# Attention's weights, copied bit for bit into rounded-kind tiles and transposed from there

## The chip, the cores and the metric

The kernel runs on one core of one Trainium2 chip. A core has TensorE (PE: matrix products and transposes, results into PSUM), VectorE (DVE), ScalarE (ACT) and GpSimd (POOL), each with its own queue of instructions, and SyncE (SP), whose queue here does nothing but issue transfers. The engines run in parallel and wait for each other by semaphores. Transfers are carried out by 16 DMA engines, whichever queue issues them. The metric is the device time of one execution in microseconds (us); lower is better.

## The reference, cut to what matters

One layer of a hybrid encoder on 1024 tokens of width 1024, all in float32. A normalised input feeds two branches, stick-breaking attention (8 heads of 64) and a gated linear recurrence (4 heads of 128); their gated sum goes through an output product, and then comes an MLP with a squared ReLU and a last normalisation. The change lies in the attention, of which the reference is:

```python
z = jnp.einsum('bhqd,bhkd->bhqk', qi, k) * scale
mask = kpos[None, :] < qpos[:, None]
log_beta = jax.nn.log_sigmoid(z)
log_rem = jnp.where(mask, log_beta - z, 0.0)
between = lax.cumsum(log_rem, axis=3, reverse=True) - log_rem
w = jnp.where(mask, jnp.exp(log_beta + between), 0.0)
return jnp.einsum('bhqk,bhkd->bhqd', w, v)
```

For a query t, the weight on key s is sigmoid(z_ts) times the product of (1 - sigmoid(z_tj)) over the keys j between s and t.

## The kernel before, in words

Everything is kept in float32, and most matrix products are built from a "rounded kind" of float32 (`F32R`): a number is split into a rounded high part and a low rest, and three products of the parts (`three`, L121 in the profile) stand for one full-precision product. A tile of the rounded kind has 4 bytes per element, like float32; an engine that writes such a tile rounds the values, and a transfer through a float32 view of it does not. In the profile's rows both kinds are often printed as f32.

The attention runs as 64 items, one for each of 8 heads (h) and 8 blocks of 128 queries (qb, in the order 7, 0, 6, 1, 5, 2, 4, 3). Item (h, qb) has nk = 128 (qb + 1) keys. It passes four steps, written two items apart from each other in the main loop:

1. `scores`: TensorE multiplies queries and keys into PSUM (`z`, 256 to 512 columns at a time, short ones padded to 256), and ScalarE takes two sigmoids of it, `rm` (L753) and `bt` (L756). GpSimd clears one column of `bt` (L757).
2. `weights`: VectorE scans `rm` backwards, which makes the running product (L775), and multiplies `bt` by it (L157). `bt` now holds the weights. For qb = 7 this is done in two parts, the upper 512 columns first (`cut`).
3. `turn`: TensorE transposes `bt` block by block, 128 x 128, against an identity matrix into PSUM banks `pw` (L124), up to four blocks a bank, 36 blocks a head, 288 in all. ScalarE copies each bank into `wT` (`hi_copy`, L144).
4. `values`: once a head's eight items are turned, TensorE multiplies `wT` with V into `po` (L121).

In iteration i of the main loop the program writes `weights` of item i + 1, `scores` of item i + 2, then some "fill" (the projections of later heads and of the recurrence: `pjqk`, `pjv`, `pji` and others, L121), then `turn` of item i. So a multiply of step 2 stands about one and a half items ahead of the transposes that need it. On TensorE the attention's blocks form one lane ("main") and the projections another ("fill"): within a lane the order is fixed, and a fill block may not run ahead of more than two main blocks. Beyond that a planner lays out each engine's order by the program's priorities and by when it reckons that an instruction is ready.

Weights for the projections come by `load` (L129) on SP's queue, in an order of their own; each waits for one of two buffers, which comes free when VectorE has split the weight before (L149). GpSimd's queue issues the small copies `QH<-QH` and `QL<-QL` (L661), which move 64 partitions of a tile to the other 64 inside the SBUF, and the transfers of the output weights (`tw`, L1195).

Tiles of up to 512 columns come from a pool of 10, wider ones from a pool of 40 slots of 4 KB per partition; a tile is given back after its last use, and a later one that finds no free slot waits.

Of the kernel before, what the change touches and what calls it, by code (L numbers as in the profile page):

```python
# [9 lines left out]
F32 = mybir.dt.float32  # L10
F32R = mybir.dt.float32r
# [8 lines left out]
P = 128  # L20
# [19 lines left out]
def kernel(  # L40
# [19 lines left out]
    nc = tc.nc  # L60
# [7 lines left out]
    cpool = ctx.enter_context(tc.tile_pool(name="consts", bufs=1))  # L68
# [6 lines left out]
    def slot(name, dt=F32):  # L75
        return spool.tile([P, 1024], dt, tag="s", name=name)

    def slot_n(name, n, dt=F32):

        if n <= 512:  # L80
            return hpool.tile([P, 512], dt, tag="h", name=name)
        return slot(name, dt)

    def bank(name):
        return psum.tile([P, 512], F32, tag="p", name=name)
# [12 lines left out]
    def after(ins, earlier):  # L98
        if earlier is not None and earlier.ins is not ins.ins:
            tc.add_manual_dep(ins.ins, earlier.ins.name, NOSYNC, reason="issue order")  # L100
        return ins

    def open_block(name):
        cur[0] = name
        lane = lanes[name]
        lane.gates = (lane.last,)
        if name == "main":
            lane.ends.append(lane.last)
        else:
            ends = lanes["main"].ends  # L110
            lane.gates += tuple(ends[-AHEAD : len(ends) - AHEAD + 1])

    def pe(ins):
        lane = lanes[cur[0]]
        for g in lane.gates:
            after(ins, g)
        lane.last = ins
        return ins
# [4 lines left out]
    def transpose(dst, src):  # L123
        return pe(nc.tensor.transpose(dst, src, ident))  # L124
# [18 lines left out]
    def hi_copy(dst, src):  # L143
        hi_last[0] = after(in_turn("act", nc.scalar.copy(dst, src)), hi_behind[0])  # L144
# [11 lines left out]
    def mul(out, a, b):  # L156
        return nc.vector.tensor_tensor(out=out, in0=a, in1=b, op=ALU.mult)  # L157
# [4 lines left out]
    ident = cpool.tile([P, P], F32, tag="ident", name="ident")  # L162
# [505 lines left out]
    def v_job(quad):  # L668
        unit = v_unit(quad)
        return st.add(  # L670
            [unit], lambda: token_steps(f"pjv{quad}", unit, xn, range(NT), v_epilogue(quad))
        )
# [51 lines left out]
    for h in range(1, NHS):  # L724
        j_qk[h] = proj_jobs([qk_item(h)], xn)
        if h == 4:
            v_job(1)

    QB_ORDER = (7, 0, 6, 1, 5, 2, 4, 3)
    items = [(h, qb) for h in range(NHS) for qb in QB_ORDER]  # L730
    zs, wTt, seen = {}, {}, {}
# [33 lines left out]
    def weights(h, qb):  # L765

        nk = (qb + 1) * P
        bt, rm = zs[h, qb]  # L770
        cut = qb == NT - 1
        parts = ((512, nk - 1), (0, 512)) if cut else ((0, nk - 1),)
        for i, (a, b) in enumerate(parts):
            rr = rm[:, a:b][:, ::-1]
            nc.vector.tensor_tensor_scan(  # L775
                out=rr,
                data0=rr,
                data1=bits[:, 1024 - nk + a : 1024 - nk + b][:, ::-1],
                initial=rm[:, b : b + 1] if i else 0.0,
                op0=ALU.mult,  # L780
                op1=ALU.max,
            )
            weighted[0] = mul(bt[:, a:b], bt[:, a:b], rm[:, a:b])

    def turn(h, qb, between):

        open_block("main")
        bt, rm = zs.pop((h, qb))
        qc, par = qb // 2, qb % 2
        nkb = 2 * qc + 2  # L790
        if (h, qc) not in wTt:
            wTt[h, qc] = [
                slot_n(f"wT{h}_{qc}_{k0}", 256 * min(nkb - k0, 4)).rearrange(
                    "p (k q) -> p k q", q=256
                )
                for k0 in range(0, nkb, 4)
            ]
        tiles = wTt[h, qc]
        qs = slice(par * P, (par + 1) * P)
        order = list(enumerate(tiles))  # L800
        for i, t in order[::-1] if qb == NT - 1 else order:
            n = min(qb + 1 - 4 * i, 4)
            if n <= 0:
                continue
            if qb == NT - 1 and i == 0:
                between()
                open_block("main")
            pw = bank(f"pw{h}_{qb}_{i}")
            for kb in range(n):
                s0 = (4 * i + kb) * P  # L810
                transpose(pw[:, kb * P : (kb + 1) * P], bt[:, s0 : s0 + P])
            hi_copy(t[:, 0:n, qs], pw[:, : n * P].rearrange("p (k q) -> p k q", q=P))
            turn_hi[0] = hi_last[0]
        seen[h] = seen.get(h, 0) + 1
        return (h,) if seen[h] == NT else None
# [1290 lines left out]
    st.advance(11, j_qk[0])  # L2106
    scores(*items[0])
    weights(*items[0])
    st.advance(1, j_qk[0])
    scores(*items[1])  # L2110
# [7 lines left out]
    for i, it in enumerate(items):  # L2118
        if i + 1 < len(items):
            weights(*items[i + 1])  # L2120
        if i + 2 < len(items):
            st.finish(j_qk[items[min(i + 4, len(items) - 1)][0]])
            scores(*items[i + 2])
        if i % 2 == 1:
            next(wsums, None)
        want = n_first + (i + 1) * (n_fill - n_first) // len(items)
        st.advance(want - done, j_hg[1])
        done = want
        before = ready.popleft() if ready else None

        def between():
            if before:
                values(*before)

        r = turn(*it, between)
        if i == len(items) - 2:
            attended[0] = weighted[0]
        if it[1] != NT - 1:
            between()
        if r:  # L2140
            ready.append(r)
# [127 lines left out]
```

## Time and profile before

| | us |
|---|---|
| median of 3 runs | 1431.91 (1429.53 to 1432.1) |
| the profiled execution | 1431.78 |
| its span, first to last instruction | 1430.0 |
| attention stage in it | 50 to 306 |

The profile's page gives the busy time of each engine, the span in 40 slices, the transfers by queue, the chain that ended last, and the costliest groups of instructions. A group's row names line, engine, operation, output tile and input tiles, shape and count, then total busy time, mean duration in ns, and how long the engine stood idle ahead of such an instruction. A matmul's duration holds the time that it takes to pass through the array, which overlaps the next one; how fast they follow each other is read from their starts.

### The profile page before, as it was taken

To read this page: it belongs to the slowest core of one execution; us is meant where nothing else is said; L and a number is where in the kernel's file an instruction comes from. 1 tells how busy PE (TensorE), PEld (TensorE's weight loads), DVE (VectorE), ACT (ScalarE), POOL (GpSimd) and SP (SyncE) were. 2 spreads that over 40 slices of the span, in tenths; PEclk is the share of its full clock that TensorE was granted. 3 is DMA by queue.
4 is the path that set the end of the run, shared out by engine and by line. 5 is a ranking of instruction groups with operands and counts; after the bars stand their busy time and mean duration, and the time that the engine had idled before them with its cause. 6 is when DMAs were issued, how large, how long until landed. Compare 5 with 4: busy or idle time off the path is not lost. (4 is left out here: it accounts for less than half of the span.)

```text
span 1430.0 us, 22381 instructions
## 1 busy us (share of the span) xinstructions
PE 1415.6 (99%) x8806; PEld 1189.1 (83%) x8806; DVE 1000.7 (70%) x1320; ACT 667.6 (47%) x1180; POOL 138.3 (10%) x283
## 2 busy tenths in 40 slices
PE   9999999999999999999989999999999999999998
PEld 8889888987888888888878888888888888888886
DVE  6577677655535677788758897766666758668765
ACT  7566676643322354432344764454444443524343
POOL 3121121110001022000010300000000000000042
PEclk9999999999999999999999999999999999999999
DMA  7235154312203458744487505444446974776725
GB/s 214 47 93 128 27 93 85 67 36 82 84 16 109 114 180 234 235 155 162 162 258 250 177 30 199 160 137 143 143 161 229 341 270 152 273 274 243 279 96 181
DMA packets 157920, 225.87 MB, mean 158 GB/s; under 512 B 25676, under 2 KB 93816, under 8 KB 157816
## 3 DMA queue, kind: packets, MB, share of 16 engines
q1 hardware_dynamic: 142552, 183.29, 38.1%
q0 software_dynamic: 11520, 34.61, 9.7%
q10 hardware_dynamic: 3744, 6.56, 1.2%
q8 instruction: 69, 1.13, 0.3%
q14 instruction: 35, 0.29, 0.1%
HBM read 162.55 MB, written 61.87 MB: 157 GB/s over the span
## 5 line engine op out<-in xcount | busy, mean ns | idle before, releaser
L775 DVE TENSOR_TENSOR_SCAN rm<-rm,bits 128x511 f32<-128x511 f32 (+7 forms) x72 | 87.9, 1225 | 47.7 <-ACT rm L753 47.6
L144 ACT CAST whid<-w 128x1024 fp32r<-128x1024 f32 x30 | 31.6, 1053 | 154.7 <-PE pm L121 86.8
L121 PE MATMUL pm<-wlod,sh 128*128 128x512 f32 x240 | 93.5, 390 | 0.0
L121 PE MATMUL pm<-whid,sh 128*128 128x512 f32 x240 | 93.4, 389 | 0.0
L121 PE MATMUL pm<-whid,sl 128*128 128x512 f32 x240 | 93.4, 389 | 0.0
L121 PE MATMUL pm<-tl,sh 128*128 128x512 f32 (+1 forms) x210 | 81.3, 387 | 0.0
L121 PE MATMUL pm<-th,sl 128*128 128x512 f32 (+1 forms) x210 | 81.3, 387 | 0.0
L121 PE MATMUL pm<-th,sh 128*128 128x512 f32 (+1 forms) x210 | 81.3, 387 | 0.0
L149 DVE TENSOR_TENSOR wlod<-w,whid 128x1024 fp32r<-128x1024 f32 x30 | 36.7, 1223 | 58.2 <-ACT whid L144 58.1
L149 DVE TENSOR_TENSOR sl<-sa,sh 128x1024 fp32r<-128x1024 f32 x56 | 68.2, 1218 | 0.5 <-ACT sh L144 0.5
L144 ACT COPY wT<-pw 128x512 f32<-128x512 f32 (+2 forms) x96 | 43.8, 484 | 45.5 <-PE pw L124 42.3
L144 ACT CAST sh<-sa 128x1024 fp32r<-128x1024 f32 x56 | 57.3, 1047 | 5.5 <-DMA sa<-ad 3.9
L1918 POOL TENSOR_SCALAR fss<-fss 128x1 f32<-128x1 f32 x8 | 4.5, 562 | 562.2 <-ACT fsc L1913 561.6
L157 DVE TENSOR_TENSOR bt<-bt,rm 128x511 f32<-128x511 f32 (+7 forms) x72 | 49.5, 690 | 9.1 <-ACT bt L756 3.0
L121 PEld LDWEIGHTS pm<-wlod,sh 128*128 128x128 f32 x240 | 45.0, 188 | 9.7 <-DVE wlod L149 0.4
L121 PEld LDWEIGHTS pm<-whid,sh 128*128 128x128 f32 x240 | 45.1, 188 | 9.4
L121 PEld LDWEIGHTS pm<-whid,sl 128*128 128x128 f32 x240 | 45.0, 188 | 9.4
L121 PE MATMUL pX<-sql,t1h 128*128 128x512 f32 x128 | 50.1, 391 | 0.1
L121 PE MATMUL pX<-sqh,t1l 128*128 128x512 f32 x128 | 49.9, 389 | 0.0
L121 PE MATMUL pX<-sqh,t1h 128*128 128x512 f32 x128 | 49.8, 389 | 0.0
L753 ACT ACTIVATE rm<-z 128x511 f32<-128x511 f32 (+4 forms) x96 | 48.3, 507 | 1.7 <-PE z L121 1.4
L756 ACT ACTIVATE bt<-z 128x512 f32<-128x512 f32 (+3 forms) x96 | 48.5, 507 | 1.2 <-PE po L121 0.9
(907 smaller groups left out, 4335.4 us busy)
## 6 DMA issues: line engine op xcount, KB each, us to landing
w<-in_w_ff_dram SPq DMA_DIRECT2D x72, 512.0 KB, 4.9
sa<-ad SPq DMA_DIRECT2D x56, 512.0 KB, 6.5
ad<-a SPq DMA_DIRECT2D x32, 256.0 KB, 4.2
ad<-s SPq DMA_DIRECT2D x16, 512.0 KB, 5.2
tw<-in_w_out_dram POOLq DMA_DIRECT2D x24, 256.0 KB, 4.3
x<-in_x_dram SPq DMA_DIRECT2D x8, 512.0 KB, 8.5
xnl<-xnh POOLq DMA_DIRECT2D x8, 512.0 KB, 9.4
pr<-pd SPq DMA_DIRECT2D x8, 512.0 KB, 6.2
```

The costliest lines, as they stand in the source:

```text
L121: return pe(nc.tensor.matmul(*a, **k))
L144: hi_last[0] = after(in_turn("act", nc.scalar.copy(dst, src)), hi_behind[0])
L149: nc.vector.tensor_tensor(out=dst, in0=src, in1=hi.bitcast(F32), op=ALU.subtract),
L157: return nc.vector.tensor_tensor(out=out, in0=a, in1=b, op=ALU.mult)
L753: nc.scalar.activation(rm[:, s0 + c0 - 1 : s0 + m - 1], z[:, c0:m], AF.Sigmoid, scale=-0.125)
L756: nc.scalar.activation(bt[:, s0 : s0 + e], z[:, :e], AF.Sigmoid, scale=0.125)
L775: nc.vector.tensor_tensor_scan(out=rr, data0=rr, data1=bits[:, 1024 - nk + a : 1024 - nk + b][:, ::-1], initial=rm[:, b : b + 1] if i else ...
L1918: nc.gpsimd.tensor_scalar(out=ssq, in0=ssq, scalar1=1.0 / D, scalar2=EPS, op0=ALU.mult, op1=ALU.add)
```

## The change

A second identity, `ident_r`, of the rounded kind is made once by ScalarE. At the end of `weights`, a tile `wr` of the rounded kind is taken, and one transfer on SP's queue (two for qb = 7, upper part first) copies `bt` into it, through a float32 view of `wr`. `turn` no longer reads `bt`: it transposes blocks of `wr` against `ident_r` into a rounded view of the same `pw` bank. The copies out of `pw` and all that follows are as before. `bt` and `rm` have their last use in `weights`.

```diff
+    ident_r = cpool.tile([P, P], F32R, tag="ident_r", name="ident_r")
+    nc.scalar.copy(ident_r, ident)
...
             weighted[0] = mul(bt[:, a:b], bt[:, a:b], rm[:, a:b])
+        wr = slot_n(f"wr{h}_{qb}", nk, F32R)
+        for a, b in ((512, nk), (0, 512)) if cut else ((0, nk),):
+            nc.sync.dma_start(wr[:, a:b].bitcast(F32), bt[:, a:b])
+        zs[h, qb] = wr
 
     def turn(h, qb, between):
 
         open_block("main")
-        bt, rm = zs.pop((h, qb))
+        wr = zs.pop((h, qb))
...
             for kb in range(n):
                 s0 = (4 * i + kb) * P
-                transpose(pw[:, kb * P : (kb + 1) * P], bt[:, s0 : s0 + P])
+                pe(
+                    nc.tensor.transpose(
+                        pw[:, kb * P : (kb + 1) * P].bitcast(F32R), wr[:, s0 : s0 + P], ident_r
+                    )
+                )
```

## The prediction

> **What bounds the kernel now.** I read the page first (busy shares, slices), then the busy times of the attention stage, then the groups of instructions in it, then single instructions in order of time.
>
> ```profile
> span 1430.0 us, 22381 instructions
> PE 1415.6 (99%) x8806; PEld 1189.1 (83%) x8806; DVE 1000.7 (70%) x1320; ACT 667.6 (47%) x1180; POOL 138.3 (10%) x283
> ...
> 50.00:306.00 256.00, 256.00 (x1682) 221.43 (x1682) 185.48 (x223) 168.88 (x399) 42.99 (x125) 1.00 0.36 75
> ...
> L124 PE MATMUL pw<-ident,bt 128*128 128x128 f32 x288 | 43.3, 273 | 0.0
> ```
>
> The third row is the stage from 50 to 306 us, in which all 64 attention items run; its columns are the length, then busy time and count of PE, PEld, DVE, ACT and POOL, the granted clock, the DMA share and GB/s. TensorE is busy for all 256.00 of 256 us at clock 1.00, VectorE for 185.48, ScalarE for 168.88. So TensorE bounds the stage, and time taken from it there should come off the end, as long as nothing else makes it wait. The last row is what the change touches: 288 transposes of `bt` (36 blocks for each of 8 heads), no idle time before them. Their 43.3 us of busy time is not their price, because matmuls overlap. The price is the step from one start to the next:
>
> ```profile
> 57.98 0.39 PE L121 MATMUL pjqk<-xnh,wqk1h 128*128 128x512 f32 x1
> 58.21 0.39 PE L121 MATMUL pjqk<-xnl,wqk1h 128*128 128x512 f32 x1
> ...
> 58.67 1.03 PE L124 MATMUL pw<-ident,bt 128*128 128x128 f32 x8
> ...
> 157.14 0.28 PE L121 MATMUL pjv<-wv1h,xnh 128*128 128x256 f32 x1
> 157.26 0.28 PE L121 MATMUL pjv<-wv1l,xnh 128*128 128x256 f32 x1
> ...
> 366.20 1.72 PE L121 MATMUL pkv<-v,pp 128*128 128x128 f32 x14
> ```
>
> Columns: start, duration, instruction. Eight transposes take 1.03 us, one alone 0.273: (1.03 - 0.273) / 7 = 0.108 us each (four in a row elsewhere, 0.60 us, give 0.109). 288 x 0.109 = 31.4 us of TensorE. The rounded-kind matmuls (`pjqk`, `pjv`; the trace prints them as f32) step 0.23 us at 512 columns and 0.12 at 256: 0.11 us for 256 columns, 0.43 ns a column, and about 0.01 us beside that. The transposes move 128 columns in 0.108, 0.84 ns a column: twice as long. That is what the change is after.
>
> **The change, part by part.**
>
> *The transposes.* Same count, same tile, but both operands of the rounded kind. No row shows such a transpose, so I bound it. Below: the columns at the rounded rate and nothing else, 128 x 0.43 = 0.055 us. Above, if the rounded kind brings that kind's slower weight load and this sets the step, the nearest row is `pkv`, full-precision 128-column matmuls with such loads: (1.72 - 0.275) / 13 = 0.111 us. The loads:
>
> ```profile
> L124 PEld LDWEIGHTS pw<-ident,bt 128*128 128x128 f32 x288 | 34.5, 140 | 6.7 <-issue 0.9 <-DVE QL L149 0.2 <-DVE osb L862 0.2
> L121 PEld LDWEIGHTS pji<-wi0h,xnl 128*128 128x128 f32 x64 | 12.2, 191 | 0.0
> L121 PEld LDWEIGHTS pkv<-v,pp x56: 187/192/192, 366.0 to 547.5; 128*128 128x128 f32 x56
> L121 PE MATMUL pkv<-v,pp x56: 270/275/275, 366.2 to 547.7; 128*128 128x128 f32 x56
> ```
>
> (Last two rows: durations as min/median/max.) A load of the same 128 columns takes 140 ns ahead of a transpose and 191 to 192 ahead of the others. The new instruction shares its operation with the 0.109 row and its kind with the 0.055 rate; being near to both, I take the middle, 0.083 us. It saves 288 x (0.109 - 0.083) = 7.5 us. Ends: 288 x 0.054 = 15.6 us saved, 288 x 0.002 = 0.6 us lost.
>
> *The copies.* 72 transfers on SP's queue, one for each multiply (two where `cut`): 288 x 64 KB = 18.9 MB, bit for bit from `bt` to `wr`. SP computes nothing, so issuing costs no engine. But each stands between the multiply (L157) that ends the weights and the transposes that need them, and its time to landing must fit into the slack there. I paired all 72 multiplies (first end at 54.1, last at 300.1 us) with the transposes of their item (58.7 to 305.3), in order: the slack runs from 2.37 to 11.88 us, median 6.0; 4 are under 3.3, 8 under 4.4, 23 under 5.4. The tightest two and a usual one:
>
> ```profile
> 106.69 0.81 DVE L157 TENSOR_TENSOR bt<-bt,rm 128x639 f32<-128x639 f32 x1
> ...
> 110.81 0.67 DVE L157 TENSOR_TENSOR bt<-bt,rm 128x511 f32<-128x511 f32 x1
> ...
> 168.03 0.83 DVE L157 TENSOR_TENSOR bt<-bt,rm 128x639 f32<-128x639 f32 x1
> ...
> 110.30 0.71 PE L124 MATMUL pw<-ident,bt 128*128 128x128 f32 x5
> ...
> 113.85 0.60 PE L124 MATMUL pw<-ident,bt 128*128 128x128 f32 x4
> ...
> 174.68 0.49 PE L124 MATMUL pw<-ident,bt 128*128 128x128 f32 x3
> ```
>
> 110.30 - 107.50 = 2.80; 113.85 - 111.48 = 2.37; 174.68 - 168.86 = 5.82 us. How long does a copy take?
>
> ```profile
> DMA packets 19854, 19.09 MB, mean 77 GB/s; under 512 B 7344, under 2 KB 15930, under 8 KB 19834
> ...
> QH<-QH POOLq DMA_DIRECT2D x14, 128.0 KB, 2.2
> ...
> wqk6r<-in_w_in_dram SPq DMA_DIRECT2D x2, 256.0 KB, 6.5
> ...
> wga0r<-in_w_in_dram SPq DMA_DIRECT2D x1, 512.0 KB, 3.8
> ...
> DMA to landing us min/median/max: 2.2/2.2/5.4
> ```
>
> The first four rows are of 58 to 306 us (the last column is us to landing), the fifth is of all transfers that touch `QH`. `QH<-QH` is the nearest: inside the SBUF, 128 KB, 2.2 us. The quietest load of 512 KB lands in 3.8. A line through both gives 2.7 us for 256 KB, 3.0 for 320, 3.3 for 384, 3.5 for 448. Against each item's own slack only the two tightest and one of 3.25 are late, by 0.3, 0.2 and 0.05 us: 0.6 us together. That is the low end. The stage's traffic doubles (19.09 MB before), and 110.9 us is just when `wqk6r` takes its 6.5 us, so the tightest item will land late by more; with 1.4 us for that I take 2.0 us of waiting. If every copy took 5.4 us, as the slowest `QH` did, the 23 items with less slack would lack 24.4 us in all (23 x 5.4 less their slacks, 99.8): the high end, since a TensorE that waits gives the next items time.
>
> *The queue it passes through.* Ahead of a copy on SP may stand a prefetched weight load that waits for its buffer:
>
> ```profile
> SPq L129 <- DVE wq1l L149: 30.5, 1, 30.5
> ...
> SPq L129 <- DVE wqk3l L149: 26.9, 1, 26.9
> ...
> 124.12 0.99 SPq L129 DMA_DIRECT2D wqk7r<-in_w_in_dram  x2
> 126.04 1.95 SPq L129 DMA_DIRECT2D wf0r<-in_w_in_dram  x1
> ...
> 181.18 0.37 SPq L129 DMA_DIRECT2D wq0r<-in_w_in_dram  x1
> ```
>
> These waits look dangerous, but SP stands there only because it ran ahead. In the program's order each such load comes after the instruction that it waits for, with two of the L157 multiplies between at the most; a copy behind it needs a multiply later on the same VectorE. I cost it at nothing; without that order a single such wait would be 20 us and more. The other way round, the loads now wait behind copies, so behind multiplies; they are issued a whole projection job ahead (the loads at 124.12 and 126.04 us are followed by the next at 181.18), and some us later do no harm. If the cover failed, ScalarE's split of that weight would be late next, then the fill matmuls.
>
> *Tiles.* `wr` takes one more tile per item, but `bt` now comes free when the copy lands and no longer when the transposes end. Both are held only while the copy flies, some 3 us. Late in the stage the 40 slots are full, and a new `bt` already waits for an older one's transposes:
>
> ```profile
> POOL bt L757 <- PE pw L124: 11.5, 1, 11.5
> ...
> L144 ACT COPY wT<-pw x96: 260/565/611, 59.4 to 305.6; 128x512 f32<-128x512 f32 x48, 128x128 f32<-128x128 f32 x16, 128x384 f32<-128x384 f32 x16, 128x256 f32<-128x256 f32 x16
> ```
>
> (First row: waits from 235 to 282 us, total, times, longest; second: all copies out of `pw`, min/median/max in ns.)
>
>
> TensorE is busy through that wait, so nothing now; what it costs if the cover goes is in the second rival. *The identity copy* is one ScalarE instruction of some 0.26 us (128 columns, as the smallest `wT` copies), once, on an engine idle for a third of the stage: nothing.
>
> **Sum.** The profiled execution took 1431.78 us (span 1430.0 and 1.8 around it), 0.13 under the median of 1431.91. 1431.8 - 7.5 + 2.0 = 1426.3 us. What cannot be told from no change is about 0.2%, 2.9 us: under 1429.0 is faster, over 1434.8 slower.
>
> **Rivals.** *One pass, fully.* The step is 0.055 to 0.06 us, and the wait stays: 1431.8 - 14.8 + 2.0 = 1419 us. For it: every rounded row in the trace goes at 0.43 ns a column. Against it: a bit-for-bit transpose must carry all 32 bits.
>
> *The transposes gain nothing.* Either all 32 bits need the two turns they take today, or the weight load sets the step at 0.111 us: 1431.8 + 0.6 + 2.0 = 1434.4 us, from 1432 to 1437, at the edge of slower. For it: the rounded kind's 191 ns loads. Against it: 140 ns for a load of the same bytes shows that a transpose's load differs. The Trainium skill, "TensorE: Matmul & The Clock Gate", section "LDWEIGHTS (loading the stationary operand)", has a load take its columns over 1.2 GHz, 107 ns here, and speaks for this rival; in its section "Terms" it calls transpose mode 4x faster for FP32 on weight loads, which speaks against it. The trace shows the short load of the f32 transpose, and cannot show that of the rounded one.
>
> *The copies come late (slower).* Place: the items that follow a big load or a projection's evacuation, as at 107 to 118 us. Price: at 4.4 us per copy the lacking slacks of the 8 tightest add up to 7.5 us, which eats the whole gain; from there on it loses, and at 5.4 us it is 1431.8 - 7.5 + 24.4 = 1449 at the most, some 1440 where half is won back by later slack. Held `bt` tiles in the full pool push the same way, since a late sigmoid makes a late multiply. For it: 6.5 us beside `wqk6r`, and 5.4 for one `QH`. Against it: 2.2 us is also the median. The Trainium skill, "DMA: Bandwidth & Descriptors", section "Issuing engines are not separate DMA queues", says that transfers issued from different engines share the same 16 DMA engines and interleave; by that rule SP's copies do meet POOL's transfers, and the 5.4 us row agrees.
>
> *A narrow rounded matmul is slow.* The kernel pads `z` to 256 columns (L121 `z` has no narrower row), as if less were no cheaper. If 128 columns fell to the full-precision rate, two records of 0.111 us: 288 x (0.222 - 0.109) = 32.5 us, 1466 us. Nothing in the trace shows a rounded matmul under 256 columns, so it can't be excluded.
>
> **How the numbers follow.** Forecast 42% (own range 1419 to 1430.5), full single pass 13%, no gain in the transposes 22%, late copies 14%, slow narrow kind 8%. Faster: 85% of the forecast and the single pass, 0.48. Same: the rest of the forecast and over half of the no-gain case, 0.20. Slower: the rest, 0.32. The range, 1417 to 1440, takes in the single pass, the no-gain case and the milder half of the late copies, and leaves out the slow narrow kind.
>
> **What would show it.** The step between `pw` starts: 0.083 right, 0.055, 0.11 or 0.22 a rival. The time to landing of `wr<-bt`: under 3.6 us right. TensorE's idle time before `pw`: 0 now, 2 us forecast; over 7 makes the third rival true. If the stage shrinks by the saving but the end does not move, I was wrong on TensorE as the bound; if weight splits wait for their loads, on SP's queue.

## The result: slower by 12.6 us

The changed kernel took 1443.33 us (median of 4 runs, 1442.83 to 1448.91); the kernel before, run beside it, took 1430.72 (4 runs, 1429.38 to 1432.1). The ratio is 1.0096, with a 95% interval of 1.0083 to 1.0109. That is 12.6 us slower, where 5.5 us faster was forecast, and outside the range of 1417 to 1440. Of the rivals, "the copies come late" (1440 to 1449) holds it.

### The profile after

First the page, then the busy times by stretch, with columns as in the prediction: length, PE, PEld, DVE, ACT and POOL, granted clock, DMA share, GB/s.

```profile
span 1441.4 us, 22689 instructions
...
PE 1413.5 (98%) x8806; PEld 1185.3 (82%) x8806; DVE 1000.3 (69%) x1320; ACT 668.0 (46%) x1181; POOL 132.3 (9%) x283
```

```profile
50.00:318.00 268.00, 254.72 (x1673) 217.71 (x1671) 185.00 (x223) 168.86 (x398) 42.95 (x125) 0.99 0.54 141
...
230.00:240.00 10.00, 10.00 (x49) 8.56 (x50) 4.49 (x6) 6.26 (x15) 0.86 (x3) 0.85 0.33 70
250.00:260.00 10.00, 7.61 (x66) 5.79 (x65) 3.50 (x3) 3.18 (x7) 1.09 (x5) 1.00 0.50 132
290.00:300.00 10.00, 9.81 (x80) 8.15 (x80) 5.56 (x8) 5.16 (x14) 1.88 (x6) 0.83 0.44 88
```

TensorE was busy for all 256 us of the stage before. Now the stage ends 13 us later and TensorE stands idle for 268.00 - 254.72 = 13.3 us of it. The granted clock, 1.00 throughout the stage before, falls to 0.85 and 0.83 in two of the slices. What the idle time waits for, and who else waits (the waits from 50 to 320 us: total, times, longest):

```profile
POOL bt L760 <- DMA wr<-bt: 34.0, 4, 10.9
...
PE pw L819 <- DMA wr<-bt: 11.6, 9, 3.2
...
ACT rm L756 <- DMA wr<-bt: 8.1, 2, 5.9
...
ACT bt L759 <- DMA wr<-bt: 5.6, 2, 5.4
...
PE pw L819 <- ACT bt L759: 1.7, 1, 1.7
...
SPq L129 <- DVE wq0l L149: 8.4, 1, 8.4
```

All ten waits of TensorE stand ahead of `pw`, nine of them for a copy by these rows (11.6 and 1.7 make up the 13.3 us). By the single records the tenth, 1.65 us at 103.68 us, is for one too: its copy landed at 103.54, and in each of the eight waits whose copy's landing the trace tells the transposes begin 0.14 us after it.

The transposes themselves, in groups and in order of time; the answering rows of before stand beside them, for the two `z` matmuls that follow each group:

```profile
L819 PEld LDWEIGHTS pw<-ident_r,wr x288: 137/140/183, 58.4 to 318.2; 128*128 128x128 f32 x144
L819 PE MATMUL pw<-ident_r,wr x288: 220/248/342, 58.7 to 318.2; 128*128 128x128 f32 x144
```

```profile
58.66 0.80 PE L819 MATMUL pw<-ident_r,wr 128*128 128x128 f32 x8
...
59.48 0.28 PE L121 MATMUL z<-KS,QL 128*128 128x256 f32 x1
...
62.35 0.22 PE L819 MATMUL pw<-ident_r,wr 128*128 128x128 f32 x1
...
62.70 0.39 PE L121 MATMUL z<-KS,QL 128*128 128x512 f32 x1
```

```profile
59.66 0.28 PE L121 MATMUL z<-KS,QL 128*128 128x256 f32 x1
...
62.53 0.27 PE L124 MATMUL pw<-ident,bt 128*128 128x128 f32 x1
...
62.87 0.39 PE L121 MATMUL z<-KS,QL 128*128 128x512 f32 x1
```

The step is (0.80 - 0.22) / 7 = 0.083 us, where it was 0.108. But from a group's start to the second `z` behind it, eight transposes take 59.48 - 58.66 = 0.82 us (0.99 before), and a single one 0.35 (0.34 before). So a group of one gains nothing: what is saved inside a group is in part lost on the way out of it, where the weight loads of the two `z` matmuls follow each other in 0.11 us in both kernels (59.37 after 59.26 here, 59.54 after 59.43 before). There are 71 groups in the order of TensorE, with 288 - 71 = 217 steps inside them. The group of eight gives 217 x 0.026 = 5.6 us as a first estimate.

The copies, in the transfers from 58 to 318 us (last column: us to landing), and over all of them:

```profile
DMA packets 29552, 37.27 MB, mean 143 GB/s; under 512 B 8474, under 2 KB 19733, under 8 KB 29529
...
tw<-in_w_out_dram POOLq DMA_DIRECT2D x23, 256.0 KB, 4.4
wr<-bt SPq DMA_DIRECT2D x22, 256.0 KB, 4.0
wr<-bt SPq DMA_DIRECT2D x8, 448.0 KB, 6.5
wr<-bt SPq DMA_DIRECT2D x8, 384.0 KB, 4.5
wr<-bt SPq DMA_DIRECT2D x8, 320.0 KB, 3.3
...
wr<-bt SPq DMA_DIRECT2D x7, 64.0 KB, 4.0
```

```profile
DMA to landing us min/median/max: 1.8/2.9/8.6
```

The stage's traffic has doubled. The copies take 4.0 us at 256 KB and 6.5 at 448, where 2.7 and 3.5 were reckoned; these are medians of the copies whose landing the trace tells, 40 of 72, and the slowest took 8.6 us. It is the slowest that cost most. Paired with their items, four waits (3.23, 2.40, 2.35 and 0.60 us, 8.6 of the 13.3) stand at items that had 6.35 to 8.5 us of slack in the kernel before, whose median was 6.2 (the prediction reads 6.0). The copies of three of them took 8.1 to 8.6 us, one of these a copy of only 64 KB; the fourth isn't told. The items with under 4.1 us of slack before have four of the waits, 3.8 us, and the tightest of all, with 2.37, has none. The longest wait shows how (in order of time):

```profile
217.10 1.09 DVE L157 TENSOR_TENSOR bt<-bt,rm 128x895 f32<-128x895 f32 x1
219.52 1.21 DVE L149 TENSOR_TENSOR wq0l<-wq0r,wq0h 128x1024 fp32r<-128x1024 f32 x1
...
220.43 0.91 POOL L1206 DMA_DIRECT2D tw<-in_w_out_dram  x1
220.79 0.37 SPq L129 DMA_DIRECT2D wi0r<-in_w_in_dram  x1
...
221.06 1.19 POOL L1206 DMA_DIRECT2D tw<-in_w_out_dram  x1
221.39 7.41 SPq L789 DMA_DIRECT2D wr<-bt  x3
...
229.95 1.10 PE L819 MATMUL pw<-ident_r,wr 128*128 128x128 f32 x7 [3.23 <-DMA wr<-bt]
```

The multiply ends at 218.19. SP is held by the load `wi0r`, which waits for the split `wq0l` (219.52 to 220.73), so the copy, the first of the three in its row, is issued only at 221.39, 3.2 us late. It then flies together with that load of 512 KB and two `tw` transfers of 256 KB, lands after 8.4 us, and TensorE has stood still for 3.23 us.

**Where 13.0 us come from.** The last `pw` starts 13.0 us later. Steps saved, -5.7 us (first experiment); TensorE idle, +13.3; two slices at 0.85 and 0.83 of the clock and a bit of the one before them, 1.5 + 1.7 + 0.2 = +3.4. That makes 11.0. Another 1.6 us lie at the same ten waits: idle time is counted from the end of the last matmul's row (0.39 us at 512 columns), while in the flow the next one starts after 0.23. From start to start the ten steps ahead of a wait are 14.9 us longer than in the first experiment, not 13.3. 0.4 us are left. After the stage 1.6 us come back (the span grew by 11.4).

The copies don't slow the engines' own work: VectorE is busy for 185.00 us of the stage (185.48 before) and ScalarE for 168.86 (168.88).

### The profile page after: what moved, and what is told of

The parts are those of the page before. It is cut to its first block, busy times and chain, and to the rows that moved or that the text cites. A ratio compares the mean times of both kernels' runs of the same rounds, so it can differ in the third digit from the quotient of the medians.

```text
span 1441.4 us, 22689 instructions
## 1 busy us (share of the span) xinstructions
PE 1413.5 (98%) x8806; PEld 1185.3 (82%) x8806; DVE 1000.3 (69%) x1320; ACT 668.0 (46%) x1181; POOL 132.3 (9%) x283
```

## The experiments

The theory now is that the rounded transposes save what they should, and that the copies land too late for some items, because they share the DMA engines with `tw` and the weight loads. The rivals are that the rounded transposes cost something that the steps don't show, that the copies are held up in SP's queue, and that the fuller pool of tiles decides. In the expectations below, "the stage" ends with the last `pw`: 305.2 us before, 318.2 after.

### Rounded transposes without copies

`bt` is itself a tile of the rounded kind; ScalarE and VectorE round as they write it, so the low bits of the weights are left out.

```diff
-        bt, rm = slot_n(f"bt{h}_{qb}", nk), slot_n(f"rm{h}_{qb}", nk)
+        bt, rm = slot_n(f"bt{h}_{qb}", nk, F32R), slot_n(f"rm{h}_{qb}", nk)
...
-            weighted[0] = mul(bt[:, a:b], bt[:, a:b], rm[:, a:b])
-        wr = slot_n(f"wr{h}_{qb}", nk, F32R)
-        for a, b in ((512, nk), (0, 512)) if cut else ((0, nk),):
-            nc.sync.dma_start(wr[:, a:b].bitcast(F32), bt[:, a:b])
-        zs[h, qb] = wr
+            weighted[0] = mul(bt[:, a:b], bt[:, a:b].bitcast(F32), rm[:, a:b])
+        zs[h, qb] = bt
```

> No copies: the tile bt itself is of the rounded kind, ScalarE and VectorE write it rounded, and the rounded-kind transposes read it. It leaves out the low bits of the weights. Theory 'late copies' (the transposes save about 4 us net, all the loss is TensorE waiting for transfers): 1426.5 us, 4 under the kernel before, no idle time of TensorE ahead of pw. Rival 'the transposes themselves' (the exposed weight load after each group, or another price of the rounded kind, is what costs): 1432 us or more, not faster than before.

Measured: 1425.09 us (before beside it 1431.33), ratio 0.9958 (0.9944 to 0.9972). Its groups and stage:

```profile
L816 PE MATMUL pw<-ident_r,bt x288: 218/247/282, 58.4 to 299.5; 128*128 128x128 f32 x144
```

```profile
50.00:302.00 252.00, 252.00 (x1701) 217.66 (x1701) 184.85 (x223) 169.50 (x399) 43.12 (x125) 1.00 0.37 77
```

The last `pw` comes at 299.5 us instead of 305.2, with TensorE busy throughout. The first part of the change is worth 5.7 us in the stage and 6.2 in the whole. The copies therefore cost some 18 us. The single records give the 5.7 us in two parts: the 217 steps inside the groups take 16.3 us in all where they took 24.0 before, 7.7 us less (0.075 us a step for 0.111, both with some longer steps among them), and the 71 ways out of a group, from its last `pw` to the second matmul behind it, take 22.6 us for 20.4, 2.1 us more.

### Copies without rounded transposes

```diff
-        wr = slot_n(f"wr{h}_{qb}", nk, F32R)
+        wr = slot_n(f"wr{h}_{qb}", nk)
...
-            nc.sync.dma_start(wr[:, a:b].bitcast(F32), bt[:, a:b])
+            nc.sync.dma_start(wr[:, a:b], bt[:, a:b])
...
+                transpose(pw[:, kb * P : (kb + 1) * P], wr[:, s0 : s0 + P])
```

> The 72 copies stay, but into float32 tiles, and the transposes are the full-precision ones of before. Theory 'late copies': about 1445 us (the 13 us of waiting and about 3 us of lost clock on top of the kernel before; a little less than that where slower transposes give the copies more time). Rival 'the transposes themselves': 1431 to 1434 us.

Measured: 1445.52 us (before 1431.33), ratio 1.0098 (1.0078 to 1.0119), last `pw` at 320.2 us. Its waits, and a slice with a lowered clock:

```profile
PE pw L124 <- DMA wr<-bt: 10.6, 7, 3.5
```

```profile
130.00:140.00 10.00, 8.04 (x55) 8.07 (x55) 4.03 (x5) 4.01 (x11) 0.65 (x3) 0.83 0.65 194
```

The loss is there without any rounded transpose: it is the copies'. It is 14 us and not the full 18. Of the difference, 2.7 us are waiting (10.6 us against 13.3), as the slower transposes would leave the copies a little more time; the rest isn't assigned.

### The copies on GpSimd's queue

```diff
-            nc.sync.dma_start(wr[:, a:b].bitcast(F32), bt[:, a:b])
+            nc.gpsimd.dma_start(wr[:, a:b].bitcast(F32), bt[:, a:b])
```

> As the changed kernel, but the copies are issued from GpSimd's queue. Theory 'behind the weight loads' (a copy that is issued on SP just after a load must let that load's rows go first): TensorE's waiting ahead of pw falls under 6 us, 1430 to 1436 us. Rival 'shared DMA engines' (any traffic slows a copy, whichever queue it is on): 10 us of waiting or more, 1440 to 1450 us; GpSimd's own tw transfers now stand ahead of the copies.

Measured: 1442.89 us (before 1431.33), ratio 1.0083 (1.0057 to 1.011), which the interval doesn't tell from the changed kernel's. Waits from 50 to 325 us, and the copies' landing:

```profile
PE pw L819 <- DMA wr<-bt: 11.3, 6, 3.3
PE pji L121 <- DVE q L157: 0.5, 1, 0.5
```

```profile
DMA to landing us min/median/max: 1.9/2.8/6.2
```

The copies wait elsewhere, and as long. The queue that issues them isn't what makes most of them late. This is what the Trainium skill says in "DMA: Bandwidth & Descriptors", section "Issuing engines are not separate DMA queues": transfers of different issuers run on the same 16 engines. The trace agrees, with 11.8 us of waiting on one queue and 13.3 on the other. GpSimd's queue has the `tw` transfers on it, so this run alone doesn't clear the queue; the one with both moves, below, does.

### The transfers of `tw` moved to the stage's end

```diff
         if i + 2 < len(items):
             scores(*items[i + 2])
-        if i % 2 == 1:
-            next(wsums, None)
...
                 if next(g, StopIteration) is not StopIteration:
                     going = True
+                    if h > 0:
+                        next(wsums, None)
```

> As the changed kernel, but the 32 tw transfers of GpSimd's queue are issued after the attention stage. Theory 'shared DMA engines': the waiting falls by half or more, 1433 to 1437 us. Rival 'behind the weight loads': the waiting stays above 9 us, 1440 to 1443 us.

Measured: 1438.37 us (before 1431.33), ratio 1.0047 (1.0032 to 1.0062), last `pw` at 309.7 us. The waits, and the longest one in order of time:

```profile
PE pw L819 <- DMA wr<-bt: 8.8, 5, 6.1
```

```profile
295.29 4.08 SPq L789 DMA_DIRECT2D wr<-bt  x2
...
295.64 4.14 POOL L1206 DMA_DIRECT2D tw<-in_w_out_dram  x8
...
309.34 0.72 PE L819 MATMUL pw<-ident_r,wr 128*128 128x128 f32 x4 [6.07 <-DMA wr<-bt]
```

Two thirds of the 8.8 us are one wait. Eight `tw` transfers were issued within 4.1 us around the issue of the last copy (the second of the two in the first row, issued at 295.29 + 4.08 - 0.46 = 298.91), and its transposes began 10.4 us after its issue. The other four waits add up to 2.7 us. Neither forecast came true: the waiting fell by a third and not by half, and the time lies between the two ranges. The rows suggest that the theory holds and that the move was too short, which the next kernel tests.

### The transfers of `tw` well behind the stage

As above, with `h > 1` in place of `h > 0`, and each transfer ordered behind an instruction of the later recurrence rather than one of the attention:

```diff
-                    after(nc.gpsimd.dma_start(tw[i][rs], src[rs], accum_op=op), lastsel[0])
+                    after(nc.gpsimd.dma_start(tw[i][rs], src[rs], accum_op=op), last_power[0])
```

> As the changed kernel, but the tw transfers are issued only well after the attention stage (with the earlier kernel with them moved, eight of them still fell on its end and one copy waited 6 us for them). Theory 'shared DMA engines': waits ahead of pw of about 3 us in all, 1428 to 1431 us. Rival 'the weight loads on the same queue': 8 us of waits or more, 1436 us or more.

Measured: 1452.33 us (before 1431.06), ratio 1.0154 (1.0136 to 1.0172), but the stage ends at 302.4. Its waits in the stage, and the copies in the transfers from 58 to 318 us:

```profile
PE pw L819 <- DMA wr<-bt: 1.7, 3, 0.6
PE pw L819 <- DVE k L894: 0.7, 1, 0.7
```

```profile
wr<-bt SPq DMA_DIRECT2D x22, 256.0 KB, 2.3
wr<-bt SPq DMA_DIRECT2D x8, 448.0 KB, 2.7
wr<-bt SPq DMA_DIRECT2D x8, 384.0 KB, 2.6
```

With `tw` out of the stage, the same copies of 256 to 448 KB on the same queue land in 2.3 to 2.7 us instead of 4.0 to 6.5, and 2.4 us of the 13.3 us of waiting are left. The weight loads are all still there, so it is the company of `tw` that makes most copies late. (The copies of 64 KB gain less, 3.6 us for 4.0.) Whether copies and `tw` meet in the DMA engines or in what lies behind them, no run separates.

The time misses the forecast by over 20 us. It is no measure here, since `tw` is now late for what follows: waits at other places, 470 to 570 us, cost it more than the stage won.

The control is the same move in the kernel before, without copies. (In its expectation `e6_tw_after` is the kernel just shown; `e7_both` and `e8_pool_tw_after` are the two with `tw` behind the stage that are shown below.)

> The kernel before, without copies, with the transfers of tw moved behind the stage as in e6_tw_after. It tells whether the 20 us that e6_tw_after, e7_both and e8_pool_tw_after lost after 470 us are the price of that move alone. Theory: yes; the stage ends at 305 us as before, the waits of TensorE between 470 and 570 us are there too, some 17 us, and the time is 1448 to 1453 us. Rival: they come from the copies in some way; then this is 1431 us.

Measured in a single run: 1453.44 us, last `pw` at 305.4 us, and these waits from 470 to 570 us:

```profile
PE sl L121 <- DVE pp L157: 10.9, 2, 6.6
PE pkv L121 <- ACT pp L1073: 5.1, 1, 5.1
```

So the later loss comes with the move alone, without any copy, and beside this control the stage of the changed kernel is 3.0 us shorter, not 13 longer.

Both moves together, `tw` behind the stage and the copies on GpSimd's queue:

> Copies on GpSimd's queue and tw after the stage, so the copies stand behind no large transfer on their queue. Theory 'behind the weight loads' as the rest of the loss: waits under 1 us, 1425 to 1427 us, less than with the copies on SP and tw after the stage. Theory 'shared DMA engines' alone: the same as with the copies on SP, within 3 us.

Measured: 1455.62 us (before 1431.06), ratio 1.0174 (1.0156 to 1.0193); last `pw` at 305.0 us, 3.3 us of waiting in the stage, where the queue theory expected under 1. GpSimd's queue is no better than SP's where `tw` is gone, either. (Its time is 3.3 us above that of the kernel with `tw` alone moved, where the other theory said within 3.)

### The multiplies one item earlier

Iteration i now writes `weights` of item i + 2 and `scores` of item i + 3: every copy has an item's more time, and `tw` stays where it is. The weights are copied bit for bit, as in the change.

```diff
-        if i + 1 < len(items):
-            weights(*items[i + 1])
+        if i == 0:
+            weights(*items[1])
+            scores(*items[2])
         if i + 2 < len(items):
+            weights(*items[i + 2])
+        if i + 3 < len(items):
             st.finish(j_qk[items[min(i + 4, len(items) - 1)][0]])
-            scores(*items[i + 2])
+            scores(*items[i + 3])
```

> As the changed kernel, but the weights and scores of an item are written one item earlier in the loop, so each copy has some 4 us more before its transposes. Theory 'late copies': TensorE's waits ahead of pw fall from 13 us to 3 or less, 1426 to 1431 us, faster than the changed kernel by 12 or more. Rival 'full slots' (one more item in flight holds two more tiles, and ScalarE and GpSimd then wait for copies to give tiles back): the stall moves to them and 1437 us or more remain.

Measured: 1428.05 us (before 1431.06), ratio 0.998 (0.997 to 0.9991). Waits from 50 to 325 us, landing, and the stage:

```profile
PE z L121 <- DMA QL<-QL: 1.1, 1, 1.1
PE pw L819 <- ACT bt L759: 0.2, 1, 0.2
```

```profile
DMA to landing us min/median/max: 1.9/3.3/7.2
```

```profile
50.00:302.00 252.00, 250.44 (x1678) 215.73 (x1678) 184.31 (x223) 167.75 (x398) 44.02 (x124) 1.00 0.56 150
```

The slack from multiply to transposes has grown from a median of 6.2 us in the kernel before to 8.75, and TensorE no longer waits for a copy. The last `pw` comes at 301.5 us. On the whole the copies land no sooner (median 3.3 us, 2.9 in the changed kernel), but the slow ones do: 4.0 us at 448 KB instead of 6.5, 3.3 at 256 KB instead of 4.0. Of the 37 copies whose landing this trace tells, only one would have been late with the slack of the changed kernel, by 1.6 us; the other 35 aren't told. So the order works, but how much of that is the longer slack, and how much that the copies meet other company at their new places, isn't separated.

More tiles are held than in the changed kernel, and the waits for tiles are as long (`bt` on GpSimd waits 36.1 us for copies, the sigmoids on ScalarE 12.2), and yet it gains; so the fuller pool doesn't decide.

With `tw` behind the stage as well:

> Both at once: one item earlier, and tw after the stage. If late copies are the whole loss, TensorE waits no more ahead of pw and the time is that of the kernel without copies, 1425 to 1427 us, some 5 under the kernel before. If copies cost something beside their lateness (slots, ports), 1430 us or more.

Measured: 1449.46 us (before 1431.06), ratio 1.0133 (1.0117 to 1.0149): the forecast of 1425 to 1427 is missed by the same loss after 470 us. The last `pw` comes at 300.0 us and one wait of 0.3 us is left in the stage: all but 0.5 us of what the transposes save is then kept.

### Three kernels side by side: order, copies, fewer copies

The kernel before with that order alone, the copies in that order again (`e5_deeper` in the expectations is the kernel with the multiplies one item earlier), and the copies for blocks 3 to 7 only:

> The kernel before, without copies, with the order of e5_deeper alone: weights and scores one item earlier. It tells what of e5_deeper's 3.0 us comes from the order and what from the rounded transposes. Theory: the kernel before has no wait of TensorE ahead of pw in the stage, so an earlier order has nothing to give it; the stage ends as before, at 305 us, and the time is 1431 us (1430 to 1433). Rival: the order itself gains (or costs) by other waits, by up to the 3.0 us of e5_deeper: 1428 us with a stage end at 302, and then the copies with rounded transposes are worth nothing even when their waiting is covered.

> The kernel of e5_deeper once more, beside the kernel before with the same order and beside copies for the large groups alone. The theory that the rounded transposes save some 5.8 us in the stage, and that an item's more time covers the copies, expects 1428 us again (1427 to 1429.5) and a last pw at 301.5 us.

```diff
+        zs[h, qb] = bt
+        if qb < 3:
+            return
         wr = slot_n(f"wr{h}_{qb}", nk, F32R)
...
+                if qb < 3:
+                    transpose(dst, src)
+                else:
+                    pe(nc.tensor.transpose(dst.bitcast(F32R), src, ident_r))
```

> The order of e5_deeper, but only the weights of queries from block 3 on are copied and transposed as the rounded kind (48 of 72); those of blocks 0 to 2 are transposed directly, as before. By the steps measured, a group of n transposes gains n x 25 ns less 46 ns that leaving the group costs more, so groups of one lose 21 ns, of two gain 4 ns, of three gain 29 ns: leaving the small ones out changes the stage by under 0.5 us, and a third of the copies is gone from the transfers. Theory: the same as e5_deeper within 1 us, 1427 to 1429 us. Rival: the number of transfers itself still costs TensorE or the other streams something in e5_deeper; then this is faster by over 1 us, 1425 to 1427.

| kernel | us (before 1431.48) | ratio | 95% | last `pw` |
|---|---|---|---|---|
| order alone, no copies | 1431.87 | 1.0002 | 0.9993 to 1.0011 | 305.8 |
| order and copies | 1428.08 | 0.9972 | 0.9964 to 0.9981 | 301.1 |
| order, copies from block 3 on | 1426.52 | 0.996 | 0.9948 to 0.9973 | 301.4 |

The order gives nothing by itself. Copies and rounded transposes in it are worth 3.8 us, 4.7 in the stage. The third kernel's time lies in the range of the rival, that the number of transfers costs something even here. But its interval overlaps the second's and its stage ends no sooner; the difference lies in waits near the end of the profiled executions (4.3 us there against 6.4), which no copy touches. So fewer copies do as well as all of them; that they do better isn't shown. Both are faster than the kernel before and than the changed one.

## Why the prediction was wrong

**TensorE bounds the stage: right.** What it saves comes off the end when nothing makes it wait (1425.09 us), and what it waits goes on top.

**The step of 0.083 us: right, by luck. The saving of 7.5 us: too large by a quarter.** The 0.083 was the middle of two bounds, with no mechanism for it; what sets the step stays open. The group of eight gives the same figure, but as a mean: by the medians of all records the first step of a group is 0.060 us and the others are 0.085. What the sum left out is the way out of a group. It counted 288 equal steps; the 217 inside the groups saved 7.7 us, and the 71 ways out cost 2.1 us more than before. By the medians, the way from the last `pw` to the second `z` grew by 22 to 46 ns, by the width of `z`. Measured: 5.7 us.

**The waiting of 2.0 us: wrong, and this is the step that failed.** It priced a copy by two of the quickest transfers at hand, 2.2 us for 128 KB and 3.8 for 512. As a price without `tw` that was even high (2.3 us for 256 KB and 2.7 for 448, with `tw` gone). But in the stage as it is, the copies meet `tw`, and take medians of 4.0 to 6.5 us at 256 to 448 KB and 8 us and more at the slowest. The prediction saw that the traffic would double, and allowed 1.4 us for it. Measured: 13.3 us.

It also looked for late copies only at items with little slack. Over half of the waiting, 8.6 us, came where the slack was usual or more; there the copies, as far as their landing is told, took 8.1 us and more, over the 5.4 us of the prediction's worst case. The third rival had the mechanism right, late copies beside other transfers, and its total came close; but at the place that it named, 107 to 118 us, TensorE waited for 0.16 us only, and it got 14% for its chance, because the median `QH` of 2.2 us was set against it. That median was the wrong witness. The rows against it stood in the same view of the kernel before: `wqk6r`, 256 KB, 6.5 us, and two that the prediction doesn't show, another kind of transfer but the company that the copies would meet:

```profile
tw<-in_w_out_dram POOLq DMA_DIRECT2D x23, 256.0 KB, 4.4
...
wf0r<-in_w_in_dram SPq DMA_DIRECT2D x1, 512.0 KB, 7.7
```

**The queue costs nothing: wrong at one place.** The argument was that a load which stands ahead of a copy waits for nothing that comes after the copy's own multiply. That took VectorE's order to be the program's. At 217 us VectorE ran the multiply ahead of the split, so SP stood there with the load in hand for 3.2 us after the multiply's end. From the rows: issued at once, a copy of 8.4 us would have landed at about 226.6, just when TensorE ran dry (229.95 - 3.23 = 226.7); issued late but in 2.7 us, at 224.1. By this reckoning it took both, the queue and the company, to make that wait. The kernel with `tw` well behind the stage agrees: there the same load holds the same copy for the same 3.2 us, the copy takes 5.4 us, and TensorE waits for 0.74 us in place of 3.23. Elsewhere in the stage no copy that TensorE waited for was issued more than 0.6 us after its multiply. A kernel with that one load elsewhere wasn't tried.

**Tiles cost nothing as long as TensorE is busy: the cover did go.** `bt` waits for the copies on GpSimd (34.0 us) and the sigmoids on ScalarE (13.7 us), where before the waits for older transposes came to 23.1 us in two on GpSimd and 0.3 on ScalarE. That late copies make late sigmoids and so late multiplies is argued, not shown. In the kernel with the multiplies one item earlier these waits are as long (36.1 and 12.2 us), and there they cost TensorE nothing.

**Not in any term: the clock.** After two of the waits TensorE ran at half its clock for 3.4 us, +3.4 us in all.

## What to carry to other kernels

A new transfer on a path that must not wait should be priced by the transfers that already fly in that stage, not by the quiet ones, and its slowest landings, not their median, set against the usual slack. If it is late, try to give it time by issuing its producer earlier: one item earlier turned +12.6 us into -3.0, with the same transfers. And a cheaper step counts only where the instruction behind it can start sooner: count the steps inside groups, and price the way out of a group by itself.

## What the runs showed that I had not expected

The granted clock falls after waits much shorter than a stage. After 3.23 us of idle TensorE (at 229.95) the slice has 0.85, after 2.35 us (290.19) 0.83, and where the copies were kept without rounded transposes after 1.96 us (131.96) 0.83; yet after 2.40 us (254.81) it stays at 1.00. A slice of 10 us at 0.83 costs 1.7 us, so a wait of 2 us can cost nearly twice its length.

The traces' clock records tell the two kinds apart. The clock changes only at points of a fixed grid, 3.41 us apart: in the changed kernel it is 0.50 from 229.56 to 232.97 and from 291.00 to 294.41, and from the first drop to the second are 18 such steps. What counts is how long TensorE was idle within one step of the grid. Up to the first drop at 229.56 it was 2.84 us, up to the second 2.35; the wait of 2.40 us was cut by the grid into 1.04 and 1.36. Over all fourteen traces, each of the 46 steps at full clock with 1.96 us or more of idle time was followed by half clock, and none of the 5756 with 1.92 or less. The Trainium skill, "TensorE: Matmul & The Clock Gate", in its part on the clock gate, has the clock halve after an idle window of about 3.4 us; here the length agrees, but a step that was idle for 1.96 us of its 3.41 was enough, and 0.83 over 10 us agrees with half speed for 3.4 of them (1 - 0.5 x 0.34 = 0.83).

A rounded transpose of 128 columns steps in 0.085 us behind another (0.060 for the first step of a group), between the 0.055 that 128 columns would take at the rate of the rounded matmuls and the 0.109 of the full-precision transpose. It does so whether its tile holds copied bits or rounded values (0.085 and 0.084), and its weight load stays at the 140 ns of the full-precision transpose, not the 191 ns of the rounded matmuls.
